# Stick-breaking attention: the values become the stationary operand, and half of the later weight copies go to another engine

## The chip, the cores and the metric

One Trainium2 chip, of which the kernel uses one core. The metric is the time of one execution in device microseconds (us), the median of several runs. Five engines work side by side, each through its own instructions in order: TensorE (PE; its weight loads are shown as PEld), VectorE (DVE), ScalarE (ACT), GpSimd (POOL) and SyncE (SP), which here only issues transfers.

## The reference

One layer: a hybrid of two sequence mixers, then a mixture of 16 experts. 512 tokens of 1024 features follow 16 meta tokens. What the change touches is the second mixer, stick-breaking attention with 8 heads of 64 features, which runs over blocks of 128 queries:

```python
def stick_breaking_mixer(q, k, v, norm_g):
    ...
    for blk in range(Lp // Q_BLOCK):
        z = jnp.einsum('bhqd,bhkd->bhqk', qh[:, :, start:end], kh[:, :, :end])
        mask = jnp.arange(end)[None, :] < (start + jnp.arange(Q_BLOCK))[:, None]
        log_keep = jnp.where(mask, jax.nn.log_sigmoid(-z), 0.0)
        log_a = jax.nn.log_sigmoid(z) + lax.cumsum(log_keep, axis=3, reverse=True) - log_keep
        a = jnp.where(mask, jnp.exp(log_a), 0.0)
        outs.append(jnp.einsum('bhqk,bhkd->bhqd', a, vh[:, :, :end]))
    o = jnp.concatenate(outs, axis=2).transpose(0, 2, 1, 3)
    return head_rms_norm(o, norm_g)
```

`head_rms_norm` divides each head's 64 features of a token by their root mean square. Both mixers' results, side by side, are multiplied by `w_out`; a layer norm, a router and the experts follow. All is float32.

## The kernel before, in words

The stages follow each other: the input projections with the first mixer (HGRN2) woven in, then the stick-breaking mixer with the output projection woven in, then the router, then the 16 experts, whose weights (96 loads of 1 MB) stream in from HBM. The large products are made in three: a float32 operand is split into a high part that TensorE takes in one pass and the low rest, and `mm3` (L126 to L130) multiplies high by high, low by high and high by low. So L128, L129 and L130 are the projections, the output projection and the experts; other products are plain float32, which the trace shows as two records for each matmul.

**The stick-breaking stage.** `UNITS` (L493) lists the work: first query block 3 alone (528 keys wide, with the meta tokens), then block 2 (400 wide), then blocks 0 and 1 together (144 + 272 = 416 wide). Heads go in pairs, four pairs `pr` for each unit. `sb_weights` (L498) makes one head's weights with queries on the partitions: `z` by TensorE, Abs, Exp and Ln on ScalarE (L518, L523, L524), a ReLU (L522), a reverse scan (L527) and a subtraction (L529) on VectorE, Exp on ScalarE (L530).

`sb_values` (L535) multiplies a pair's weights by the values. For each head it turns the 128x128 blocks of weights with TensorE (L543) into the one bank `tr`, VectorE copies them out as `aT` (L545: four blocks in the first unit, three in the others), and L550 has a block of `aT` as the stationary operand and 64 columns of values `svt` as the moving one, so that the result bank `o` holds queries on the partitions and features along the row. There are 12 such groups (three units of four pairs), 24 copies and 80 products.

`sb_finish` (L553) ends a group of heads and runs five times (for unit 1, for unit 2, and in unit 3 for the pairs 0 and 1, for pair 2, for pair 3): the meta tokens' part (L562), Square on ScalarE (L567), a sum over 64 features on VectorE (L569), Ln and Exp of 8 numbers a row on ScalarE (L570, L571), a multiplication on VectorE (L572), four transposes back to features on TensorE (L575), and in `mixed_parts` (L470) the high part on ScalarE (L477) and the low part on VectorE (L478). These feed the second half of the output projection, `wo_mm`.

**What sets the order.** `weave` (L68, called in L929) interleaves the steps of `stick_breaking` and `out_proj` by a ratio; a scheduler then lays the instructions out engine by engine, and each engine runs its own in that order. Large tiles `b` come from a ring of 14 buffers (`big`, L98): each new tile waits until the one 14 places before it is no longer used. The raw loads of `w_out` (L730, split on L736 and L737) and of the experts' weights (L894, split on L922 and L923) come from it. The PSUM bank `tr` has one buffer, the small tiles `t` have two (`T_BUFS`, L60).

## Time and profile before

| | us |
|---|---|
| median of 3 runs | 701.22 (699.14 to 703.21) |
| the profiled execution | 695.96 |
| its span, first to last instruction | 694.2 |
| stick-breaking stage in it (first of its score products to the last of its low parts) | about 236 to 348 |
| router and first expert's start | about 348 to 400 |
| experts | about 400 to 650 |

The profile gives, for each engine and stretch, how long the engine was busy; for each group of instructions how often it ran, how long one took, and the idle time of the engine before it with what ended that idle time. A record's time includes that until its result is out, so records of TensorE overlap: the distance from one start to the next tells what one costs. The profiled execution is 5.26 us shorter than the median of the runs.

### The profile page before, as it was taken

To read this page: it belongs to the slowest core of one execution; us is meant where nothing else is said; L and a number is where in the kernel's file an instruction comes from. 1 tells how busy PE (TensorE), PEld (TensorE's weight loads), DVE (VectorE), ACT (ScalarE), POOL (GpSimd) and SP (SyncE) were. 2 spreads that over 40 slices of the span, in tenths; PEclk is the share of its full clock that TensorE was granted. 3 is DMA by queue.
4 is the path that set the end of the run, shared out by engine and by line. 5 is a ranking of instruction groups with operands and counts; after the bars stand their busy time and mean duration, and the time that the engine had idled before them with its cause. 6 is when DMAs were issued, how large, how long until landed. Compare 5 with 4: busy or idle time off the path is not lost. (4 is left out here: it accounts for less than half of the span.)

```text
span 694.2 us, 9353 instructions
## 1 busy us (share of the span) xinstructions
PE 652.1 (94%) x3354; PEld 513.8 (74%) x3354; DVE 524.6 (76%) x836; ACT 412.4 (59%) x624; POOL 158.8 (23%) x177
## 2 busy tenths in 40 slices
PE   7999989999999999989978899999999999999983
PEld 6778867777778777778766678878778787787732
DVE  5353065675563796999779899999999999999484
ACT  5363333635262673855434778678688687698480
POOL 5210153343243100100001112333111141211301
PEclk9999999999999999999998999999999999999998
DMA  9532111011004880203567699999999999999641
GB/s 319 194 104 67 55 61 61 1 61 61 1 1 166 302 319 1 90 34 121 190 236 283 261 338 326 356 354 351 351 334 353 337 362 348 334 358 376 187 164 59
DMA packets 62451, 143.67 MB, mean 207 GB/s; under 512 B 7386, under 2 KB 7418, under 8 KB 62400
## 3 DMA queue, kind: packets, MB, share of 16 engines
q1 hardware_dynamic: 53312, 127.67, 50.9%
q0 software_dynamic: 5904, 12.82, 6.3%
q10 hardware_dynamic: 3184, 2.53, 1.2%
q8 instruction: 28, 0.46, 0.3%
q14 instruction: 23, 0.19, 0.1%
HBM read 137.01 MB, written 14.68 MB: 219 GB/s over the span
## 5 line engine op out<-in xcount | busy, mean ns | idle before, releaser
L923 DVE TENSOR_TENSOR b<-b 128x1024 fp32r<-128x1024 f32 x180 | 211.3, 1216 | 5.2 <-ACT b L922 5.1
L922 ACT ACTIVATE b<-b 128x1024 fp32r<-128x1024 f32 x180 | 177.6, 1054 | 7.8 <-PE pj L130 4.8
L128 PE MATMUL pj<-b 128*128 128x512 f32 x256 | 103.8, 407 | 2.3 <-ACT b L207 2.3
L129 PE MATMUL pj<-b 128*128 128x512 f32 x256 | 101.8, 397 | 0.5 <-DVE b L124 0.5
L130 PE MATMUL pj<-b 128*128 128x512 f32 x256 | 101.6, 398 | 0.0
L128 PE MATMUL pj<-b,xh 128*128 128x512 f32 x224 | 90.4, 404 | 0.2 <-ACT b L922 0.2
L129 PE MATMUL pj<-b,xl 128*128 128x512 f32 x224 | 88.2, 394 | 0.6 <-DVE xl L1243 0.6
L130 PE MATMUL pj<-b,xh 128*128 128x512 f32 x224 | 87.4, 408 | 0.8 <-DVE b L923 0.8
L124 DVE TENSOR_TENSOR b<-b 128x1024 fp32r<-128x1024 f32 x24 | 32.4, 1357 | 47.7 <-ACT b L339 44.0
L984 POOL DMA_INDIRECT xg<-h1d,idx x15 | 20.9, 1393 | 174.7 <-DVE gate L981 71.0
L128 PEld LDWEIGHTS pj<-b 128*128 128x128 f32 x256 | 48.3, 189 | 14.2 <-ACT b L207 2.6
L130 PEld LDWEIGHTS pj<-b 128*128 128x128 f32 x256 | 48.5, 190 | 10.6 <-issue 0.7
L129 PEld LDWEIGHTS pj<-b 128*128 128x128 f32 x256 | 48.6, 190 | 10.3 <-DVE b L124 0.9
L130 PEld LDWEIGHTS pj<-b,xh 128*128 128x128 f32 x224 | 42.6, 190 | 11.8 <-DVE b L923 3.1
L339 ACT ACTIVATE b<-b 128x1024 fp32r<-128x1024 f32 x28 | 29.3, 1059 | 35.6 <-PE pj L130 21.6
L1033 POOL DMA_INDIRECT ad<-y,idx x14 | 41.0, 2926 | 38.9 <-ACT b L922 30.4
L129 PEld LDWEIGHTS pj<-b,xl 128*128 128x128 f32 x224 | 42.5, 190 | 9.8 <-DVE xl L1243 1.0
L128 PEld LDWEIGHTS pj<-b,xh 128*128 128x128 f32 x224 | 42.8, 191 | 8.7 <-ACT b L922 1.5
L640 ACT ACTIVATE zs<-zs 128x512 f32<-128x512 f32 x28 | 17.7, 631 | 45.9 <-POOL zs L639 45.8
L122 POOL TENSOR_TENSOR b<-b 128x1024 fp32r<-128x1024 f32 x8 | 21.1, 2636 | 84.6 <-ACT b L339 65.6
L638 POOL TENSOR_TENSOR zs<-u 128x256 f32<-128x256 f32 x28 | 21.2, 756 | 59.5 <-issue 19.1
L641 DVE TENSOR_TENSOR zs<-zs,u 128x256 f32<-128x256 f32 x28 | 14.3, 510 | 21.7 <-ACT zs L640 21.6
(359 smaller groups left out, 1279.1 us busy)
## 6 DMA issues: line engine op xcount, KB each, us to landing
b<-in_w_exp_gate_dram SPq DMA_DIRECT2D x32, 1024.0 KB, 8.2
b<-in_w_exp_up_dram SPq DMA_DIRECT2D x32, 1024.0 KB, 10.2
b<-in_w_exp_down_dram SPq DMA_DIRECT2D x32, 1024.0 KB, 9.8
b<-in_w_in_dram SPq DMA_DIRECT2D x12, 1024.0 KB, 4.9
b<-in_w_out_dram SPq DMA_DIRECT2D x4, 1024.0 KB, 4.8
b<-in_x_dram SPq DMA_DIRECT2D x7, 512.0 KB, 7.6
b<-in_w_in_dram SPq DMA_DIRECT2D x4, 512.0 KB
h1d<-b POOLq DMA_DIRECT2D x4, 512.0 KB, 3.7
```

What stands on the lines that cost most here:

```text
L122: nc.gpsimd.tensor_sub(dst, src, hi)
L124: V.tensor_sub(dst, src, hi)
L128: nc.tensor.matmul(acc, ah, bh, start=first, stop=False)
L129: nc.tensor.matmul(acc, al, bh, start=False, stop=False)
L130: return nc.tensor.matmul(acc, ah, bl, start=False, stop=last)
L339: latest[0] = nc.scalar.activation(wt[:, 0], src, AF.Copy).ins
L638: nc.gpsimd.tensor_sub(xv[:, :, 0, :], ref, bv[:, :, 0, :])
L640: nc.scalar.activation(X, X, AF.Exp)
L922: latest[:] = (nc.scalar.activation(t[:, 0], raw, AF.Copy).ins, V.tensor_sub(t[:, 1], raw, f32(t[:, 0])).ins)
L923: V.tensor_sub(t[:, 1], raw, f32(t[:, 0])).ins)
L984: nc.gpsimd.indirect_dma_start(out=dst, out_offset=None, in_=h1d, in_offset=bass.IndirectOffsetOnAxis(ap=idx, axis=0), bounds_check=T - 1, ...
L1033: nc.gpsimd.indirect_dma_start(out=ad, out_offset=bass.IndirectOffsetOnAxis(ap=idx, axis=0), in_=y, in_offset=None, bounds_check=T - 1, oo ...
```

## The change

The operands of the products of weights and values change places. The 64 columns of values become the stationary operand and the block of `aT` the moving one. The first head's result goes to partitions 0 to 63 of `o` and the second head's to 64 to 127, so that `o` holds features on the partitions. The two heads' products alternate, in a fixed order (`issue_after`), and the first waits for the second head's copy. In the units whose groups have three blocks, the first head's copy is made by ScalarE (8 of the 24 copies). `sb_finish` copies `o` out at once into a large tile (`mixed_room`, two more tiles from the ring of 14), squares the copy, sums over a head's features by a product with `pair` (ones in two 64x64 blocks), takes Ln and Exp of whole rows, and multiplies. The four transposes back and VectorE's sum are gone.

```diff
--- before.py
+++ after.py
@@ -384,6 +384,11 @@
     skT, sqZ, svt = [], [], []
     vbd = att.tile([P, 512], F32, name="vbd")
 
+    pair = att.tile([P, P], F32, name="pair")
+    nc.gpsimd.memset(pair, 0.0)
+    for s in range(2):
+        nc.gpsimd.memset(pair[64 * s:64 * s + 64, 64 * s:64 * s + 64], 1.0)
+
     def ev_sk(c, acc):
         skT.append(att.tile([P, 528], F32, tag="skT", bufs=4, name="skT"))
         nc.scalar.activation(skT[c][:, NM:528], acc, AF.Copy)
@@ -466,6 +471,16 @@
 
     mixed = {}
     mixed_t, mixed_n = [None], [0]
+
+    rooms = []
+
+    def mixed_room():
+
+        if len(rooms) % 4 == 0:
+            rooms.append(big_tile(4))
+        else:
+            rooms.append(rooms[-1])
+        return rooms[-1][:, (len(rooms) - 1) % 4]
 
     def mixed_parts(src):
         width = src.shape[1]
@@ -534,7 +549,7 @@
 
     def sb_values(n, pr, prs, o, zz, qts, spans):
 
-        aTs = []
+        aTs, last = [], None
         blocks = [(m, j, a + NM + j * P) for m, (i, (a, b)) in enumerate(zip(qts, spans)) for j in range(i + 1)]
         w = len(blocks)
         for s in range(2):
@@ -542,13 +557,21 @@
             for n_, (m, j, a) in enumerate(blocks):
                 nc.tensor.transpose(p_[:, n_, :], zz[s][:, a:a + P], ident)
             aT = quad(tt("aT", AT_BUFS, 512))
-            V.tensor_copy(aT[:, 0:w], p_[:, 0:w])
+            if s == 0 and len(blocks) < 4:
+                nc.scalar.activation(aT[:, 0:w], p_[:, 0:w], AF.Copy)
+            else:
+                copied = V.tensor_copy(aT[:, 0:w], p_[:, 0:w])
             aTs.append(aT)
-        for s in range(2):
-            for n_, (m, j, _) in enumerate(blocks):
-                c_ = (m * len(prs) + n) * P + 64 * s
-                nc.tensor.matmul(o[:, c_:c_ + 64], aTs[s][:, n_, :], svt[j][:, (2 * pr + s) * 64:(2 * pr + s + 1) * 64],
-                                 start=(n == 0 and s == 0 and n_ == 0), stop=False, skip_group_check=True)
+        for n_, (m, j, _) in enumerate(blocks):
+            c_ = (m * len(prs) + n) * P
+            for s in range(2):
+                with tc.issue_after(last) if last else ExitStack():
+                    i_ = nc.tensor.matmul(o[64 * s:64 * s + 64, c_:c_ + P], svt[j][:, (2 * pr + s) * 64:(2 * pr + s + 1) * 64],
+                                          aTs[s][:, n_, :], start=(n == 0 and n_ == 0), stop=False, skip_group_check=True)
+                if last is None:
+                    tc.add_manual_dep(i_.ins, copied.ins.name, mybir.DependencyInfo(
+                        mybir.DependencyClass.Sync, mybir.DependencyReason.DATA), reason="both heads side by side")
+                last = i_.ins
 
     def sb_finish(am, o, prs, qts):
 
@@ -558,22 +581,23 @@
             nc.tensor.transpose(p_[:, m, :], am[:, m, :], ident)
         aMT = att.tile([P, 2 * P], F32, tag="aMT", bufs=1, name="aMT")
         V.tensor_copy(aMT[:, 0:len(qts) * P], p_[:, 0:len(qts)].rearrange("p a b -> p (a b)"))
-        for m in range(len(qts)):
-            nc.tensor.matmul(o[:, m * w:m * w + w], aMT[:, m * P:(m + 1) * P], vbd[:, prs[0] * P:prs[0] * P + w],
-                             start=False, stop=True, skip_group_check=True)
+        for n, pr in enumerate(prs):
+            for m in range(len(qts)):
+                c_ = (m * len(prs) + n) * P
+                nc.tensor.matmul(o[:, c_:c_ + P], vbd[:, pr * P:pr * P + P], aMT[:, m * P:(m + 1) * P],
+                                 start=False, stop=True, skip_group_check=True)
         n = len(qts) * w
-        heads = lambda ap: ap[:, 0:n].rearrange("p (h d) -> p h d", d=64)
-        t = tt(n=n)
-        nc.scalar.activation(t, o[:, 0:n], AF.Square)
-        rs = att.tile([P, 8], F32, tag="rs", bufs=2, name="rs")[:, 0:n // 64]
-        V.tensor_reduce(rs, heads(t), axis=AX.X, op=OP.add)
-        nc.scalar.activation(rs, rs, AF.Ln, scale=1.0 / 64.0, bias=eps_rms)
+        t, rs = tt(n=n), tt(n=n)
+
+        oc = mixed_room()[:, 0:n]
+        nc.scalar.activation(oc, o[:, 0:n], AF.Copy)
+        nc.scalar.activation(t, oc, AF.Square)
+        n_ = pj([P, n])
+        nc.tensor.matmul(n_, pair, t, start=True, stop=True)
+        nc.scalar.activation(rs, n_, AF.Ln, scale=1.0 / 64.0, bias=eps_rms)
         nc.scalar.activation(rs, rs, AF.Exp, scale=-0.5)
-        V.tensor_mul(heads(t), heads(o), rs[:, :, None].to_broadcast([P, n // 64, 64]))
-        p_ = pj([P, 4, P])
-        for j in range(n // P):
-            nc.tensor.transpose(p_[:, j, :], t[:, j * P:(j + 1) * P], ident)
-        hi, lo = mixed_parts(p_[:, 0:n // P].rearrange("p a b -> p (a b)"))
+        V.tensor_mul(rs, rs, oc)
+        hi, lo = mixed_parts(rs)
         for m, i in enumerate(qts):
             for n, pr in enumerate(prs):
                 c_ = slice((m * len(prs) + n) * P, (m * len(prs) + n + 1) * P)
```

How the instructions stand, with the tiles' buffer numbers. The first place is on TensorE at the beginning of unit 2, where unit 1 has just been finished. Before (`t` is the normalized result of unit 1, L511 and L513 the scores of the unit's third and fourth heads with their mask, `pj` their banks, `oT` the result `o`):

```order
L575 MATMUL pj_2199<-ident_75,t_2192 128x128 x4
L511 MATMUL pj_2213<-skT_1258,b_1797 128x400
L513 LDWEIGHTS identb_222
L513 MATMUL pj_2213<-maskb_223,identb_222 128x128
L511 MATMUL pj_2232<-skT_1258,b_1797 128x400
L513 LDWEIGHTS identb_222
L513 MATMUL pj_2232<-maskb_223,identb_222 128x128
L550 MATMUL oT_2245<-b_1572,aT_2250 128x64 x3
L550 MATMUL oT_2245<-b_1572,aT_2256 128x64 x3
```

In the changed kernel (L558 turns a head's weights, L526 and L528 are the scores):

```order
L558 MATMUL tr_2257<-ident_75,zs_2150 128x128 x3
L596 MATMUL pj_2204<-t_2199,pair_245 128x512
L526 MATMUL pj_2218<-skT_1262,b_1801 128x400
L528 LDWEIGHTS identb_222
L528 MATMUL pj_2218<-maskb_223,identb_222 128x128
L526 MATMUL pj_2237<-skT_1262,b_1801 128x400
L528 LDWEIGHTS identb_222
L528 MATMUL pj_2237<-maskb_223,identb_222 128x128
L569 MATMUL oT_2250<-aT_2255,b_1576 64x128
L569 MATMUL oT_2250<-aT_2261,b_1576 64x128
L569 MATMUL oT_2250<-aT_2255,b_1576 64x128
L569 MATMUL oT_2250<-aT_2261,b_1576 64x128
```

One product of 512 columns (L596) stands where four transposes stood, and the six products of the unit's first pair (L569, the last two not shown), which took their `aT` one after the other, alternate between the two heads' `aT` and have a result of 64 partitions by 128 columns.

The second place is on ScalarE, at the end of unit 2 (L530 is the Exp that ends a head's weights, L567 to L477 belong to `sb_finish`, L765 to the output projection, L262 and L263 to the layer norm after it, L518 is the Abs of a head of unit 3). Before:

```order
L530 ACTIVATE zs_2440<-zs_2440 128x416
L765 ACTIVATE b_2561<-z_2562 128x512
L567 ACTIVATE t_2480<-oT_2245 128x512
L765 ACTIVATE b_2561<-z_2568 128x512
L570 ACTIVATE rs_2482<-rs_2482,eps_rms_80 128x8
L571 ACTIVATE rs_2482<-rs_2482 128x8
L262 ACTIVATE mv_2586<-mv_2586,eps_ln_82 128x1
L263 ACTIVATE mv_2586<-mv_2586 128x1
L477 ACTIVATE b_2204<-pj_2487 128x512
L518 ACTIVATE t_2499<-pj_2494 128x416
```

In the changed kernel (L593 is the copy of `o`, L561 the copy of a head's turned weights, L594 Square, L597 and L598 Ln and Exp, L789 the output projection, L533 and L538 a head of unit 3, L492 the high part):

```order
L593 ACTIVATE b_2201<-oT_2250 128x512
L561 ACTIVATE aT_2550<-tr_2546 128x384
L594 ACTIVATE t_2488<-b_2201 128x512
L789 ACTIVATE b_2566<-z_2567 128x512
L789 ACTIVATE b_2566<-z_2573 128x512
L262 ACTIVATE mv_2591<-mv_2591,eps_ln_82 128x1
L597 ACTIVATE t_2489<-pj_2492,eps_rms_80 128x512
L263 ACTIVATE mv_2591<-mv_2591 128x1
L598 ACTIVATE t_2489<-t_2489 128x512
L533 ACTIVATE t_2504<-pj_2499 128x416
L538 ACTIVATE t_2504<-t_2504 128x416
L492 ACTIVATE b_2209<-t_2489 128x512
```

ScalarE has the copy of the bank and a copy of turned weights more between the end of unit 2 and the high part, its Ln and Exp are of 512 columns instead of 8, and the next head's Abs and Exp stand ahead of the high part.

The third place is on ScalarE too, where the second half of `w_out` is first split (L736; it falls into unit 2). Before, with the Abs (L518) of the unit's sixth head:

```order
L518 ACTIVATE t_2297<-pj_2294 128x400
L524 ACTIVATE t_2275<-t_2275 128x400
L530 ACTIVATE zs_2236<-zs_2236 128x400
L523 ACTIVATE t_2297<-t_2297 128x400
L736 ACTIVATE b_2391<-b_2389,cp_191 128x1024
```

In the changed kernel (L760 is the split, L533 the Abs of the unit's seventh and eighth heads, L538, L539 and L545 Exp, Ln and Exp):

```order
L533 ACTIVATE t_2345<-pj_2342 128x400
L545 ACTIVATE zs_2281<-zs_2281 128x400
L538 ACTIVATE t_2345<-t_2345 128x400
L545 ACTIVATE zs_2303<-zs_2303 128x400
L539 ACTIVATE t_2345<-t_2345 128x400
L533 ACTIVATE t_2358<-pj_2355 128x400
L760 ACTIVATE b_2396<-b_2394,cp_191 128x1024
```

The first split stands behind the Abs of the eighth head instead of that of the sixth.

## Rows read from the trace of the kernel before

**Rows 1.** Windows: us, busy of PE, PEld, DVE, ACT, POOL (count), PEclk, DMA share, GB/s.
```profile
236.00:258.00 22.00, 20.26 (x119) 15.81 (x117) 20.17 (x37) 18.80 (x42) 1.40 (x6) 1.00 0.96 380
258.00:282.00 24.00, 23.48 (x124) 17.71 (x125) 16.25 (x28) 10.32 (x21) 1.58 (x6) 1.00 0.00 1
282.00:339.00 57.00, 52.70 (x328) 43.38 (x328) 54.20 (x114) 37.77 (x78) 4.90 (x10) 1.00 0.26 93
348.00:400.00 52.00, 41.72 (x239) 35.01 (x238) 43.25 (x94) 26.68 (x36) 6.81 (x8) 0.93 0.69 260
400.00:650.00 250.00, 246.15 (x1197) 196.76 (x1196) 239.65 (x306) 191.56 (x227) 59.56 (x27) 0.99 0.98 343
```

**Rows 2.** Groups of instructions from 236 to 348 us, shapes apart.
```profile
L543 PE MATMUL tr<-ident,zs 128*128 128x128 f32 x80 | 13.1, 276 | 3.7 <-DVE aT L545 3.4 <-ACT t L518 0.3
...
L569 DVE TENSOR_REDUCE rs<-t 128x8 f32<-128x512 f32 x3 | 2.0, 683 | 0.1
...
L569 DVE TENSOR_REDUCE rs<-t 128x4 f32<-128x256 f32 x2 | 0.8, 400 | 0.0
```

**Rows 3.** Timeline of DVE: start us, us, instruction.
```profile
294.50 0.53 DVE L545 COPY aT<-tr 128x384 f32<-128x384 f32 x1
294.95 0.56 DVE L529 TENSOR_TENSOR zs<-pj,zs 128x400 f32<-128x400 f32 x1
...
307.94 0.69 DVE L569 TENSOR_REDUCE rs<-t 128x8 f32<-128x512 f32 x1
308.54 0.55 DVE L545 COPY aT<-tr 128x384 f32<-128x384 f32 x1
```

**Rows 4.** Timeline of PE: full-width float32 products and transposes.
```profile
279.65 1.50 PE L550 MATMUL oT<-b,aT 128*128 128x64 f32 x12
280.99 0.89 PE L511 MATMUL pj<-skT,b 128*128 128x400 f32 x2
...
306.14 1.12 PE L562 MATMUL oT<-vbd,aMT 128*128 128x512 f32 x2
307.10 0.49 PE L543 MATMUL tr<-ident,zs 128*128 128x128 f32 x3
...
309.99 0.64 PE L575 MATMUL pj<-ident,t 128*128 128x128 f32 x4
310.47 0.41 PE L511 MATMUL pj<-skT,b 128*128 128x144 f32 x2
```

**Rows 5.** Timeline of PE: products in strips of 32 and of 64 columns of the array.
```profile
24.61 0.39 PE L129 MATMUL pj<-b 128*128 128x512 f32 x1
24.84 0.39 PE L130 MATMUL pj<-b 128*128 128x512 f32 x1
25.15 1.07 PE L372 MATMUL z<-b,xm 128*32 128x512 f32 x8
26.15 0.50 PE L128 MATMUL pj<-b 128*128 128x512 f32 x1
...
129.74 0.68 PE L650 MATMUL z<-zs 128*64 128x64 f32 x8
```

**Rows 6.** Timeline of ACT: the last `sb_finish`, and the first split of `w_out`.
```profile
285.94 1.14 ACT L736 ACTIVATE b<-b,cp 128x1024 fp32r<-128x1024 f32 x1
...
344.12 0.39 ACT L567 ACTIVATE t<-oT 128x256 f32<-128x256 f32 x1 [5.88 <-PE oT L562]
...
346.72 0.38 ACT L477 ACTIVATE b<-pj 128x256 fp32r<-128x256 f32 x1 [0.99 <-PE pj L575]
```

**Rows 7.** Timeline of DVE: the multiplication of the last `sb_finish`.
```profile
345.77 0.42 DVE L572 TENSOR_TENSOR t<-oT,rs 128x256 f32<-128x256 f32 x1 [0.60 <-ACT rs L571]
```

**Rows 8.** Waits of ACT, 236 to 348 us: total us, times, longest.
```profile
ACT zs L530 <- DVE zs L529: 13.3, 12, 3.4
```

**Rows 9.** Timeline of SP: the loads of the second half of `w_out`.
```profile
244.28 41.00 SPq L730 DMA_DIRECT2D b<-in_w_out_dram  x2
```

**Rows 10.** Line L730, from the issue to the landing of its loads.
```profile
DMA to landing us min/median/max: 4.8/4.8/4.8
```

## The prediction

> **What bounds the kernel now.** I read the windows first, because the change touches one stage alone. The reader is to see that the engine at its limit is not the same from stretch to stretch [rows 1]. From 236 to 258 us (unit 1) VectorE is busy 20.17 of 22 us; from 258 to 282 TensorE 23.48 of 24, which is 97.8%, and VectorE only 16.25; from 282 to 339 (units 2 and 3) VectorE 54.20 of 57 and TensorE 52.70, so both are close to full, with ScalarE at 37.77. From 348 to 400 (router) VectorE leads with 43.25 of 52, and in the experts TensorE has 246.15 of 250 while the transfer engines are at 0.98. The granted clock is 1.00 up to 339, TensorE's upper level of 2.4 GHz, so nothing in the stage is priced at a lower one.
>
> Then the groups of this stage [rows 2]. They show who waits: TensorE's transposes L543 wait 3.4 us in all for VectorE's copies L545. So VectorE is the likelier limit of 282 to 339, with TensorE about 1.5 us behind it. A saving on one alone is worth little more than that; both must fall.
>
> **VectorE.** A record's duration is longer than what it costs: the copy that starts at 294.50 lasts 0.53 us, but the next operation starts at 294.95, so it costs 0.45 [rows 3]. In the same way a sum over 512 columns costs 0.60 (307.94 to 308.54) [rows 3]; the one over 256 has 400 ns on record against 683 [rows 2], and I put it at 0.31, less by the same overlap. Eight of 24 copies go to ScalarE, one for each pair of units 2 and 3; all five sums go. In the whole case this is 8 x 0.45 + 3 x 0.60 + 2 x 0.31 = 6.0 us by distance, or 8 x 0.55 [rows 3] + 2.0 + 0.8 [rows 2] = 7.2 by duration. In 282 to 339 lie six of the copies, two large sums and one small: 2.7 + 1.5 = 4.2 us. The multiplication and the low part stay, at the same size.
>
> **TensorE, the values.** A group of a narrow unit is 12 records now, from 279.65 to 280.99: 1.34 us, 0.112 each [rows 4]. A record has 64 moving columns and a stationary block of 128 columns, and its 12 loads set this distance. In the changed kernel the block moves (128 columns) and 64 columns are loaded, into one half of the array for the first head and the other half for the second. A pass of 512 float32 columns costs 0.43 us: the two of L562 run from 306.14 to 307.10, entry included [rows 4]. So 128 columns cost 0.107.
>
> Whether the two halves run side by side no row shows for 64 columns. The nearest is L372, whose strips are 32 columns wide: eight records of 512 columns, four strips by two passes, take 1.07 us [rows 5] where one full-width product of two passes takes 1.12 [rows 4]. The strips do run side by side. A change of shape costs something at its edges: L372 starts 0.31 after the record ahead of it, where 0.23 is usual for that stream, ends 0.10 before the next, which lasts 0.50 instead of 0.39 [rows 5]. With its own first load I put this at 0.34 for a group. The eight 64-column records of L650 last 0.68 in all, each with a load of its own [rows 5], so inside one strip a load is hidden. I count 0.02 for the second strip's later start: 0.13 a pair of records. A narrow group then costs 6 x 0.13 + 0.34 = 1.12 instead of 1.34, and a wide one (16 records, 1.79 by the same distance) 8 x 0.13 + 0.34 = 1.38. That is -0.22 and -0.41.
>
> The Trainium skill, page "TensorEngine Tiling (Array Packing)", section Performance Considerations, names this very exchange of the operands for a moving side of at most 64 columns; its Theoretical Speedup is up to two. By it alone, without the edges that rows 5 show, a group would as an estimate halve to 0.67, and TensorE would have 6 x 0.45 = 2.7 us less in the sum below.
>
> **TensorE, the finish.** Four transposes of L575 cost 0.48 us (309.99 to 310.47) [rows 4]. The product with `pair` is 512 columns in two passes, 0.96 by L562. So +0.48 in each of the three finishes with 512 columns, and +0.24 in the two with 256. L562 keeps its size in columns. In 282 to 339: 6 x (-0.22) + 2 x 0.48 + 0.24 = -0.1 us. TensorE is left where it was; what it gains is shorter waits for `aT`, since the first head's copy runs on another engine.
>
> **ScalarE.** It gets eight copies (0.5 us each, by VectorE's), a copy of `o` (0.4 to 0.6), and Ln and Exp of 512 or 256 columns instead of 8. With 37.77 of 57 us busy there is room for it in units 2 and 3 [rows 1]. I cost it at nothing there; the cover is ScalarE's idle time, and if the order put the copies behind something that waits, the price is that of the second rival.
>
> **The end of the stage.** In the last finish nothing covers the chain. Now it goes from the Square at 344.12 to the high part at 346.72, 2.60 us [rows 6]. Then: copy 0.39 and Square 0.39 (as the Square now), product about 0.65 (0.48 and its way out), Ln and Exp 0.39 each, multiplication 0.42 [rows 7], and some 0.3 for the signals: 2.95. So +0.35.
>
> **Loads and the ring.** `mixed_room` takes two of the 14 large buffers. The first load of the second half of `w_out` is now issued at 244.28 and the second only 41 us later [rows 9], when a buffer that the first half's weights held comes free. In the changed kernel the first one must wait in this way too, and at worst as long: until 285.3; it lands 4.8 us after its issue [rows 10], at 290.1. Its split, now at 285.94 [rows 6], would be 4.1 us late where it stands; but it stands two heads further down, which is 9 us at the mean pace of the stretch (six pairs in 57 us). Between 0 and 4.1 us; I take 0, the later place being its cover. On SP the experts' loads behind it move later too; the experts come after the router, so I cost that at nothing. POOL's memsets of `pair` stand at the program's start, where nobody waits for them.
>
> **The sum.** In 282 to 339 VectorE's part would give 4.2 us. TensorE's limit is (52.7 - 0.1) / 0.978 = 53.8 us, a gain of 3.2. I take 3.8 for the stretch, between the two, as shorter waits for `aT` also fall to TensorE. From 258 to 282 TensorE is full; it has one pair product more (+0.48) and a few of the wide groups (-0.41 each): about 0. Unit 1 itself keeps its copies on VectorE: 0. With the end's -0.35 the gain is 3.45 us. The router follows the stage and is bound by VectorE; the experts are full. So a shift of the stage's end passes on. The profiled execution of 695.96 us would become 692.5; it lies 5.26 below the median, and the median of 701.22 becomes **697.8**. Ends: all of VectorE's 7.2 us gives 694.0; a gain of 0.95 (the third rival) gives 700.3. About 0.5%, 3.5 us here, is what a measurement of this kernel can tell from no change, so the forecast lies at that border.
>
> **Rivals.**
> First, the halves don't run side by side. Then a narrow group costs 12 x 0.107 + 0.34 = 1.63, or +0.29. In 282 to 339 TensorE has 52.7 + 1.7 + 1.2 = 55.6, over 0.978 is 56.9: gain 0.1. Add about 1.1 in 258 to 282 (0.48 and 0.26 for each of two or three wide groups) and 0.65 at the end (the last group lies there too): **702.9**. For it: no row has two heads' records in halves of 64. Against: L372 [rows 5]. Chance 0.12.
>
> Second, on the other side: ScalarE runs in order, and a copy L561 stands behind an Exp of weights that waits for VectorE. Now these waits are 13.3 us in 12 times, 1.1 each [rows 8]. While the copy waits, the one bank `tr` stays full, the second head's transposes wait, and TensorE with all behind them. If all eight copies bring such a wait onto the path, 8.9 - 3.45 = 5.4 us are lost: **706.7**. It decides from 3.1 copies on, where the gain is eaten. For it: at the end of unit 2 the copy stands behind two Exps and the copy of `o`. Against: ScalarE's own waits are for VectorE, which gets lighter. Chance 0.16.
>
> Third, the loads into the halves aren't hidden. A half load is 0.056 (half of 0.112); a pair of records 0.186, a narrow group about 1.44, +0.10: TensorE has 52.7 + 0.6 + 1.2 = 54.5, over 0.978 is 55.7, gain 1.3, and 0.95 with the end: **700.3**. L650's records speak against it, but they lie in one strip [rows 5]. Chance 0.05. The Trainium skill, page "TensorE: Matmul & The Clock Gate", Part 3 (packing), says a load overlaps running products only when its row groups differ; the two heads share all rows. By that rule it is this rival that comes; no run here yet shows it for halves.
>
> Fourth, the gain is absorbed: the experts' transfers are at 0.98 [rows 1], and if they, not the stage's end, set the experts' pace, the time stays at **701.2**. Against: TensorE is as full, and later loads are released by buffers that the stage frees. Chance 0.07.
>
> **Numbers.** Forecast 0.60: 0.37 of it below 697.7 (faster by over 0.5%), 0.23 within. No overlap: 0.04 within, 0.08 slower. ScalarE: 0.02 within, 0.14 slower. Third and fourth: 0.12 within. Together 0.37, 0.41, 0.22. The range of 8 in 10 reaches from the forecast's lower end, 694.0, to 704.0, which takes in the no-overlap case and half of the way to ScalarE's; above it and below lie 0.2.
>
> **What would show it.** Right: records of L569 that start in pairs less than 0.05 us apart, a narrow group of about 1.1 us; the first head's L561 close behind its transposes; L558 hardly waiting for `aT`; VectorE some 4 us lighter in units 2 and 3; the last low part near 344.5 instead of 348; the experts as long as before. Wrong: a group of 1.6 us (first rival); ScalarE's L561 late behind Exp and TensorE idle at L558 for a bank (second); a stage that ends earlier and experts that take the difference (fourth); or a split L760 that waits for its load and holds the projection.

## The result, and the profile after

Over 20 runs each the changed kernel took 707.25 us in the median (701.96 to 711.49) and the kernel before 702.59: ratio 1.0073, 95% interval 1.0051 to 1.0095. (The ratios and the means over runs, here and below, take the runs in the faster state alone, and the ratios are not quotients of the medians.) It is slower by about 5 us, where 3.45 us less were forecast. The profiled execution of the changed kernel is 710.99 us (span 709.3), 3.7 above its median; that of the kernel before lies 6.6 below its own. So the two profiles are 15 us apart, three times what the medians are. Where a second profile of the same kernel differs, it is said.

The windows that answer to [rows 1], for the changed kernel:

```profile
282.00:339.00 57.00, 52.96 (x334) 39.86 (x331) 50.82 (x104) 42.15 (x89) 4.86 (x11) 0.97 0.27 96
348.00:400.00 52.00, 36.86 (x208) 30.92 (x207) 37.35 (x88) 21.42 (x32) 6.15 (x7) 0.83 0.60 224
400.00:650.00 250.00, 246.63 (x1204) 198.00 (x1203) 240.95 (x308) 196.04 (x231) 66.24 (x27) 0.99 0.98 345
```

VectorE has 3.4 us less to do in 282 to 339, as it should (4.2 were forecast), and TensorE is as busy as ever. The router is where the rows part: 52 us hold 36.86 us of TensorE where they held 41.72, at a granted clock of 0.83 instead of 0.93. In the experts TensorE is full in both.

**The stage.** One window over the whole stage, from the first Abs to the start of the last low part. Before:

```profile
234.64:347.14 112.50, 105.49 (x625) 84.08 (x623) 95.65 (x195) 69.50 (x146) 9.23 (x24) 1.00 0.40 147
```

The changed kernel:

```profile
236.27:349.95 113.68, 105.57 (x643) 77.93 (x641) 90.05 (x182) 76.24 (x159) 7.83 (x23) 0.98 0.40 147
```

The changed kernel with one edit behind the stage (`gather_late`, below; its instructions in the stage are the same):

```profile
234.92:347.39 112.47, 104.35 (x643) 76.67 (x641) 89.99 (x181) 76.28 (x159) 7.85 (x23) 1.00 0.40 148
```

Where the clock stays at 1.00, the stage is 112.50 us before and 112.47 after: nothing was gained and nothing lost. With one fall of the clock in it (0.98 and 0.99) it is 113.68 after, and 114.03 in the second profile of the kernel before. Before, TensorE is busy 105.49 of 112.50 us and VectorE 95.65: over the whole stage it is TensorE that is near its limit.

**The products of weights and values** themselves became much cheaper. TensorE's timeline, changed kernel, one group of unit 2:

```profile
281.26 0.22 PE L528 MATMUL pj<-maskb,identb 128*128 128x128 bf16 x1
281.41 0.88 PE L569 MATMUL oT<-aT,b 128*64 128x128 f32 x12
282.21 0.94 PE L526 MATMUL pj<-skT,b 128*128 128x400 f32 x2
```

Twelve records cost 0.80 us (281.41 to 282.21), where they cost 1.34 [rows 4] and 1.12 were forecast. The halves run side by side, and the loads are hidden. But they now wait, for the second head's copy; before, TensorE waited for copies at the turning, 3.4 us [rows 2], and that is gone but for 1.0. The waits of TensorE in the stage (total us, times, longest), changed kernel:

```profile
PE oT L569 <- DVE aT L563: 2.9, 4, 1.1
PE pj L519 <- DVE zs L544: 2.2, 4, 1.1
...
PE tr L558 <- ACT aT L561: 1.0, 2, 0.6
```

**Behind the stage.** The waits of TensorE from 350 us on, before:

```profile
PE z L970 <- ACTq L1133: 2.9, 1, 2.9
PE z L1054 <- DMA xg<-h1d,idx: 2.0, 1, 2.0
PE tr L818 <- DVE Mb L805: 1.7, 1, 1.7
```

and in the changed kernel:

```profile
PE z L994 <- DVEq L1157: 5.1, 1, 5.1
PE z L1078 <- DMA xg<-h1d,idx: 4.9, 1, 4.9
PE tr L842 <- DVE Mb L829: 2.6, 1, 2.6
```

These are the same three places: the branch behind expert 0, the first gathered rows (transposes L1054, now L1078), and the ranks of the router (L818, now L842). Together they are 6.6 us before and 12.6 after. The second profiles say the same: 3.8, 1.6 and 1.7 before, 4.9, 4.7 and 2.6 after. No line that the diff touches stands there. What changed is the order that the scheduler chose. In the kernel before no product stands among the eight transposes; in the changed one:

```order
L128 MATMUL pj<-b,xh 128x512
L1078 MATMUL z<-ident,xg 128x128
L130 MATMUL pj<-b,xh 128x512
L128 MATMUL pj<-b,xh 128x512
L129 MATMUL pj<-b,xl 128x512
L130 MATMUL pj<-b,xh 128x512
L1078 MATMUL z<-ident,xg 128x128 x7
```

and its timeline:

```profile
380.63 0.40 PE L128 MATMUL pj<-b,xh 128*128 128x512 f32 x1
385.93 0.47 PE L1078 MATMUL z<-ident,xg 128*128 128x128 f32 x1 [4.90 <-DMA xg<-h1d,idx]
386.06 0.77 PE L130 MATMUL pj<-b,xh 128*128 128x512 f32 x1
386.63 0.63 PE L128 MATMUL pj<-b,xh 128*128 128x512 f32 x1
387.05 0.63 PE L129 MATMUL pj<-b,xl 128*128 128x512 f32 x1
387.48 0.63 PE L130 MATMUL pj<-b,xh 128*128 128x512 f32 x1
387.91 1.56 PE L1078 MATMUL z<-ident,xg 128*128 128x128 f32 x7
```

Four products that were ready (`gather_late`, below, runs them ahead of the transposes without a wait) stand behind a transpose that waits for a transfer, and when they run at last, the clock is low: 0.43 us from one to the next instead of 0.23. They also stand ahead of the other seven transposes, so the gathered rows, ScalarE, VectorE and the branch come later in turn.

The order is not all of it. Four products of 0.23 us are 0.9 us of the 2.9 by which the wait for the gather grew. The rest is the gather itself: it was issued 26.5 us after the start of the last low part instead of 25.9, and took 9.5 and 9.3 us to land (first and second profile) where it took 8.0 and 8.4. Why the transfer took longer is not shown. The longer wait before the ranks delays nothing by itself: L818 and L842 both start 13.5 us after the last low part, and only less other work stands ahead of them.

From the last low part of the stage to the Silu of expert 0 it is 39.8 us before (347.14 to 386.95) and 43.4 after (349.95 to 393.31), and 39.5 and 43.1 in the second profiles. To the Silu of expert 1, behind the branch, it is 53.6 and 61.3 us (second profiles 54.8 and 61.2); 1.5 us of that come back by the Silu of expert 5.

The clock follows the idle time. Windows of four microseconds around these places, before:

```profile
361.00:365.00 4.00, 1.28 (x8) 1.01 (x9) 4.00 (x9) 0.88 (x1) 0.00 (x0) 0.89 0.00 0
365.00:369.00 4.00, 4.00 (x27) 4.00 (x26) 4.00 (x11) 0.60 (x1) 2.10 (x4) 0.69 0.32 129
...
381.00:385.00 4.00, 3.86 (x14) 3.44 (x15) 1.66 (x3) 2.45 (x4) 0.00 (x0) 0.57 1.05 402
...
389.00:393.00 4.00, 3.47 (x22) 2.94 (x23) 3.40 (x9) 1.35 (x2) 0.77 (x1) 1.00 0.44 147
```

and in the changed kernel, which is some 3 to 7 us later here:

```profile
364.00:368.00 4.00, 1.79 (x9) 1.41 (x10) 4.00 (x9) 0.00 (x0) 0.00 (x0) 0.50 0.00 0
368.00:372.00 4.00, 4.00 (x21) 4.00 (x20) 2.64 (x6) 1.27 (x2) 2.10 (x4) 0.50 0.34 136
...
392.00:396.00 4.00, 0.02 (x1) 0.00 (x0) 2.37 (x5) 3.77 (x4) 0.00 (x0) 1.00 0.01 2
396.00:400.00 4.00, 2.92 (x14) 2.36 (x15) 3.58 (x8) 0.00 (x0) 0.20 (x1) 0.50 0.37 114
400.00:404.00 4.00, 4.00 (x13) 3.18 (x12) 3.17 (x10) 2.12 (x2) 2.15 (x2) 0.64 1.02 379
```

TensorE idles before each fall, and works at the lower of its two levels (1.2 instead of 2.4 GHz) right after it. The wait at the branch (392 to 396) is followed by a fall, in both profiles of the changed kernel. The first profile of the kernel before has none there, but its second has one too (granted clock 0.60 in 392 to 396), so this fall doesn't belong to the changed kernel alone.

Each run has its span and mean clock; span times (1 - clock), the time by which the grant was short, is 14.6 us in the mean of 97 runs of the kernel before and 19.8 in 32 of the changed one, 5.2 more. What is left of the span is 685.4 and 685.8. So over all runs the loss goes with a lower grant; how much of it the falls cost can't be read from this sum, since it also counts falls in which TensorE stood idle.

### The profile page after: what moved, and what is told of

Its sections match the earlier page's. It is cut to its first block, busy times and chain, and to the rows that moved or that the text cites. A ratio compares the mean times of both kernels' runs of the same rounds, so it can differ in the third digit from the quotient of the medians.

```text
span 709.3 us, 9372 instructions
## 1 busy us (share of the span) xinstructions
PE 657.7 (93%) x3364; PEld 511.4 (72%) x3364; DVE 520.4 (73%) x823; ACT 419.2 (59%) x637; POOL 165.6 (23%) x180
## 5 line engine op out<-in xcount | busy, mean ns | idle before, releaser
L947 DVE TENSOR_TENSOR b<-b 128x1024 fp32r<-128x1024 f32 x180 | 211.4, 1218 | 5.5 <-ACT b L946 5.4
L946 ACT ACTIVATE b<-b 128x1024 fp32r<-128x1024 f32 x180 | 177.9, 1054 | 13.5 <-PE pj L130 11.9
L128 PE MATMUL pj<-b 128*128 128x512 f32 x256 | 105.9, 416 | 1.5 <-ACT b L207 1.4
L129 PE MATMUL pj<-b 128*128 128x512 f32 x256 | 103.2, 403 | 0.5 <-DVE b L124 0.5
L130 PE MATMUL pj<-b 128*128 128x512 f32 x256 | 103.6, 406 | 0.0
L124 DVE TENSOR_TENSOR b<-b 128x1024 fp32r<-128x1024 f32 x24 | 35.4, 1482 | 46.1 <-ACT b L339 42.6
L1008 POOL DMA_INDIRECT xg<-h1d,idx x15 | 24.6, 1641 | 157.3 <-DVE gate L1005 94.3
L128 PEld LDWEIGHTS pj<-b 128*128 128x128 f32 x256 | 49.6, 194 | 13.9 <-ACT b L207 1.6
L1057 POOL DMA_INDIRECT ad<-y,idx x14 | 45.7, 3265 | 56.4 <-ACT b L946 46.1
L129 PEld LDWEIGHTS pj<-b 128*128 128x128 f32 x256 | 49.8, 194 | 10.7 <-DVE b L124 0.9
L130 PEld LDWEIGHTS pj<-b 128*128 128x128 f32 x256 | 49.2, 193 | 11.2 <-issue 0.7
L130 PEld LDWEIGHTS pj<-b,xh 128*128 128x128 f32 x224 | 42.4, 189 | 10.9 <-DVE b L947 2.4
```

The lines of the kernel that those rows point to most:

```text
L124: V.tensor_sub(dst, src, hi)
L128: nc.tensor.matmul(acc, ah, bh, start=first, stop=False)
L129: nc.tensor.matmul(acc, al, bh, start=False, stop=False)
L130: return nc.tensor.matmul(acc, ah, bl, start=False, stop=last)
L946: latest[:] = (nc.scalar.activation(t[:, 0], raw, AF.Copy).ins, V.tensor_sub(t[:, 1], raw, f32(t[:, 0])).ins)
L947: V.tensor_sub(t[:, 1], raw, f32(t[:, 0])).ins)
```

## The experiments

Theory A was that the loss comes from the router's ranks alone, B that it is made by the new waits in the stage, C by the two large buffers; D, after the first four runs, that it is made at the first gather, and E that it is not.

**`cover_after`**: all products of `sf` between the last scores and the ranks.

```diff
-    for hf in range(2):
-        first_rows(hf, 1)
+    with tc.issue_after(score[0]):
+        for hf in range(2):
+            first_rows(hf, 1)
```

> The changed kernel with one edit: the 16 products of sf (L968 there) are held until the last scores of tokens 0 to 255 (L792), so that TensorE has 1.8 us of work while VectorE ranks; in the changed kernel 2 of the 16 stand there, before the change 6. Theory A (the loss is made in the router: less work in this gap, TensorE idle 2.6 us instead of 1.7, the granted clock down to 0.50, the gather and the first experts later): idle before the rank products about 1 us, clock near 1.00 from there to the first expert, and 3 to 5 us less than the changed kernel, ratio to the kernel before 0.999 to 1.003. Theory B (the loss is made in the stick-breaking stage by new waits, and the router only follows): no more than 1 us less than the changed kernel, ratio about 1.007. Theory C (two buffers less for the expert weights): as B.

Measured: 707.24 us, ratio 1.0110 (1.0065 to 1.0156). The wait before the ranks is gone from its profile, and the kernel takes no less than the changed one: theory A falls.

**`cover_before`**: the same edit in the kernel before.

> The kernel before with the same edit alone: all 16 products of sf (L944) between the last scores and the ranks, where 6 stood. Theory A: the gap of 1.7 us shrinks to under 1, the granted clock falls less often in the router, and the kernel is 1 to 3 us faster, ratio 0.996 to 0.999. Theories B and C: no difference, within 1 us.

Measured: 703.70 us, ratio 1.0022 (0.9983 to 1.0062). No difference that the interval shows; it agrees with the run above.

**`one_by_one`**: the heads' products one after the other, in the same halves of the array.

```diff
-        for n_, (m, j, _) in enumerate(blocks):
-            c_ = (m * len(prs) + n) * P
-            for s in range(2):
-                with tc.issue_after(last) if last else ExitStack():
+        for s in range(2):
+            for n_, (m, j, _) in enumerate(blocks):
+                c_ = (m * len(prs) + n) * P
```

> The changed kernel, but the two heads' products of weights and values no longer alternate: the first head's, then the second's, without a fixed order, the first not waiting for the second head's copy. If the halves of the array run side by side only where the heads alternate, a group of 12 records goes from 0.8 us or less to 1.4 or more, 12 groups 7 us of TensorE's time; where TensorE is the limit of the stage this costs 3 to 5 us (ratio 1.012). Theory B (the products' wait for both copies makes the loss, 2.9 us of TensorE in the stage): the waits for aT fall to under 1 us, and the time is the same as the changed kernel's or up to 2 us less. Theory A: the stage may end anywhere within 2 us of the changed kernel's, and the router keeps its loss, ratio near 1.007.

Measured: 709.50 us, ratio 1.0147 (1.0096 to 1.0198). TensorE's timeline of this kernel:

```profile
298.07 0.87 PE L568 MATMUL oT<-aT,b 128*64 128x128 f32 x6
298.87 0.49 PE L130 MATMUL z<-b 128*128 128x512 f32 x1
299.30 0.87 PE L568 MATMUL oT<-aT,b 128*64 128x128 f32 x6
```

Six records of one head alone cost 0.80 us, as much as twelve of both that alternate. So the two heads do run at the same time, and only where they alternate. The waits for copies fell to 0.7 us, yet the stage took 116.7 us instead of 112.5: theory B's remedy costs more than the wait.

**`before_again`** and **`after_again`**: both kernels once more, for a second profile.

> The kernel before once more, for a second profile: where the granted clock falls. If its falls are a matter of the order of the work, they come in the same places as in the first profile (360 to 370 and 380 to 390 us, none near 100 us, none in 300 to 310); if they differ from run to run at the same stalls, a single profile can't be set against another without taking out the falls. Ratio 1.000 within 0.002.

> The changed kernel once more, for a second profile: falls of the granted clock that the order of the work causes come again in the same places (361.9, 385.8 and 396.0 us in the first); the one near 99 us, where both kernels have the same instructions, may be missing. Ratio 1.007 within 0.003.

Measured: 701.86 us, ratio 1.0022 (0.9990 to 1.0054), and 707.93 us, ratio 1.0085 (1.0054 to 1.0116). The three waits are those given above, and the falls at the ranks, the gather and the branch come again in the changed kernel. The falls near 99 and 300 us come and go from profile to profile.

**`gather_late`**: the changed kernel; the transposes wait on TensorE until the products ahead of them in the program are issued.

```diff
-            transposed(1, big_tile(2, F32R))
+            with tc.issue_after(ended[0].ins):
+                transposed(1, big_tile(2, F32R))
```

> The changed kernel with one edit: the eight transposes of the first gathered rows (L1078, which wait for a transfer) are held on TensorE until the products of expert 0 that stand before them in the program are issued, as they stood before the change; in the changed kernel four of these products stand behind the first transpose. Theory D (the loss is made at the first gather, because the new stage makes the scheduler put work that is ready behind a transpose that waits): TensorE's wait for the gather falls from 4.9 us to 2 to 3, the wait of VectorE behind it from 5.0 to about 2, the granted clock doesn't fall a second time near 396 us, and the kernel is 3 to 4 us faster than the changed one: ratio 1.001 to 1.003. Theory E (the loss is made in the stage and in clock falls that have nothing to do with this place): within 1 us of the changed kernel, ratio 1.006 to 1.009.

Measured: 703.62 us, ratio 1.0040 (1.0008 to 1.0072), beside 707.93 us and 1.0085 for the changed kernel (`after_again`). TensorE's waits from 350 us on:

```profile
PE z L1078 <- DMA xg<-h1d,idx: 3.2, 1, 3.2
PE z L994 <- DVEq L1157: 3.0, 1, 3.0
PE tr L842 <- DVE Mb L829: 2.6, 1, 2.6
```

8.8 us instead of 12.6. This one edit of order, behind the stage, takes 4.3 us off the median, of the 5.8 by which the changed kernel was slower there; between the means it is 3.1 us (95%: 1.1 to 5.2) of 5.6. Theory E falls: the order at this place makes a good part of the loss. Theory D came true only in part. The wait for the gather fell to 3.2 us and not below 3, since the gather still landed 35.4 us after the last low part (34.0 before, 36.0 after). A fall of the clock remains at the branch, and in the mean of 12 runs the grant is still short by 18.7 us; the rest of the span is 683.8. So the edit took 2.0 us off the rest and only 1.1 off the short grant.

**`no_copy`**: Square and the multiplication read the bank; no large tiles.

```diff
-        oc = mixed_room()[:, 0:n]
-        nc.scalar.activation(oc, o[:, 0:n], AF.Copy)
+        oc = o[:, 0:n]
```

> The changed kernel without the copy of the result bank: Square and the multiplication read the bank itself, and no large tiles are taken for it. Its row of instructions at the first gather is that of the kernel before (no product behind a waiting transpose). Theory D: 3 to 4 us less than the changed kernel, ratio 1.001 to 1.003. Theory E: the stage decides; the copy was 0.4 to 0.6 us of ScalarE in each of five finishes and freed the bank earlier, so within 1 us of the changed kernel, ratio 1.006 to 1.009. If the two large tiles were the cause (the second half of w_out loaded 40 us later), the first split of w_out comes back to about 287 us and the stage's end 1 us earlier.

Measured: 701.46 us, ratio 1.0001 (0.9968 to 1.0034). Its stage is 112.77 us long, no shorter than the others; the order at the gather is the old one, and the loss is gone.

**`copy_small`**: the copy in a small tile, the ring of large buffers as before.

```diff
-        t, rs = tt(n=n), tt(n=n)
-        oc = mixed_room()[:, 0:n]
+        oc, t = tt(n=n), tt(n=n)
```

> The changed kernel with the copy of the result bank in a small tile instead of two large ones, Ln, Exp and the multiplication in place of the Square: the ring of large buffers is as before the change. At the first gather TensorE's row is that of the changed kernel, four products behind a waiting transpose. If the two large tiles made the loss (the second half of w_out and the experts' weights load later): 3 to 4 us less than the changed kernel, ratio 1.001 to 1.003. If the order at the gather makes it: as the changed kernel, ratio 1.005 to 1.009, though the first split of w_out comes 2 us or more earlier.

Measured: 707.14 us, ratio 1.0085 (1.0054 to 1.0116). Without the two large tiles the loss is all there. Its profiled execution, 702.01 us, is the shortest of its ten. In it four products do stand behind the first transpose, but it shows no loss at the gather:

```profile
PE z L992 <- DVEq L1155: 5.1, 1, 5.1
PE tr L840 <- DVE Mb L827: 2.6, 1, 2.6
PE z L1076 <- DMA xg<-h1d,idx: 1.8, 1, 1.8
```

The gather landed after 6.5 us, and TensorE waited 1.8 us for it, less than in the first profile of the kernel before. From the last low part to the Silu of expert 1 it is 56.6 us, against 57.5 in `gather_late` and 61.3 in the changed kernel. The stage, on the other hand, is 115.6 us long, 1.9 more than the changed kernel's with one fall of the clock in each; the copy now holds one of the two small tiles `t`, which may be why. So this run can't tell the order from the stage. Theory C falls by `gather_late`, which keeps both large tiles while most of the loss is gone. That the copy brings the new order is shown: every variant of the changed kernel that copies `o` has four products behind the first transpose (`gather_late` apart, whose edit moves them), and the two that don't copy it, `no_copy` and `no_copy_scalar`, have none. The first split of `w_out` started at 293.00 us, where the changed kernel has it at 292.94: it did not come earlier with the old ring.

**`before_split`**: the kernel before, with six ready products put behind the waiting transposes (`turned` is the first of these).

```diff
-                    mm3(acc[w], (xh[:, k, :], xl[:, k, :]), (sp[w][0][:, c_], sp[w][1][:, c_]),
-                        k == 0, k == KC - 1)
+                    with tc.issue_after(turned[0]) if turned[0] else ExitStack():
+                        ended[0] = mm3(acc[w], (xh[:, k, :], xl[:, k, :]), (sp[w][0][:, c_], sp[w][1][:, c_]),
+                                       k == 0, k == KC - 1)
+                if e == 0 and kk == 2 and k2 == 0:
+                    with tc.issue_after(ended[0].ins):
+                        transposed(1, big_tile(2, F32R))
```

> The kernel before with one edit that makes the order of the changed kernel worse than it has it: six products of expert 0 that are ready stand on TensorE behind the eight transposes that wait for the first gather (none stood there before, four in the changed kernel). Nothing in the stick-breaking stage differs. Theory D: TensorE's wait for the gather grows from 2.0 us by 1.4 (six products of 0.23), the first expert ends 2 us later, a further fall of the granted clock comes with it, and the kernel is 2 to 5 us slower than before, ratio 1.003 to 1.007. Theory E (this place is covered anyway): within 1 us, ratio 1.000.

Measured: 702.80 us, ratio 1.0031 (0.9996 to 1.0066). The wait grew from 2.0 to 3.2 us (1.6 in the second profile of the kernel before), near what was expected. The time points the same way, but the interval still holds no change at all: inconclusive by itself. Here all eight transposes still run ahead of the products, and the wait at the branch stays at 2.9 us.

**`all_vector`**: the changed kernel with all copies of turned weights on VectorE.

```diff
-            if s == 0 and len(blocks) < 4:
-                nc.scalar.activation(aT[:, 0:w], p_[:, 0:w], AF.Copy)
-            else:
-                copied = V.tensor_copy(aT[:, 0:w], p_[:, 0:w])
+            copied = V.tensor_copy(aT[:, 0:w], p_[:, 0:w])
```

> The changed kernel with all 24 copies of turned weights on VectorE. Its row of instructions at the first gather is that of the changed kernel. Theory D: the loss there stays. VectorE gets back 8 x 0.45 = 3.6 us in units 2 and 3; if VectorE sets the stage, it ends 2 to 3 us later, ratio 1.010; if the waits of TensorE for both copies set it, a copy on ScalarE or on VectorE is nearly the same, ratio 1.006 to 1.008.

Measured: 713.92 us, ratio 1.0175 (1.0125 to 1.0224). The whole stage, as above:

```profile
235.92:357.48 121.56, 109.03 (x645) 80.72 (x643) 94.15 (x190) 74.66 (x151) 7.62 (x23) 0.96 0.38 139
```

9.1 us longer than `gather_late`'s, for eight copies of 0.45, and slower than either case that was expected: TensorE idles 12.5 us instead of 8.1, and the clock falls with it (0.96).

**`before_scalar`**: the kernel before with the same eight copies on ScalarE, and nothing else.

```diff
-            V.tensor_copy(aT[:, 0:w], p_[:, 0:w])
+            if s == 0 and len(blocks) < 4:
+                nc.scalar.activation(aT[:, 0:w], p_[:, 0:w], AF.Copy)
+            else:
+                V.tensor_copy(aT[:, 0:w], p_[:, 0:w])
```

> The kernel before with the changed kernel's copies on ScalarE alone (8 of 24); its order at the first gather is that of the kernel before. TensorE waited 3.4 us for copies in the stage, and its waits in the stage are 5.3 us in all. If these waits are what VectorE's work costs in the stage, they fall by 2 to 3 us: ratio 0.996 to 0.998. If VectorE's busy share set the stretch as I had forecast, up to 4 us: ratio 0.994. If copies on ScalarE queue behind an Exp that waits for VectorE (second rival): 1 to 4 us slower, ratio 1.002 to 1.006.

Measured: 699.34 us, ratio 0.9969 (0.9939 to 0.9998): 2.5 us less than the kernel before, and the only one here whose interval lies below 1. The stage:

```profile
234.53:345.16 110.63, 105.82 (x625) 83.75 (x623) 91.90 (x187) 71.40 (x154) 8.52 (x24) 1.00 0.42 157
```

1.9 us shorter; TensorE idles 4.8 us instead of 7.0, and its waits for copies, 3.4 us before [rows 2], are 0.8 in sum.

**`no_copy_scalar`**: `no_copy` with both heads' copies on ScalarE in units 2 and 3.

```diff
-            if s == 0 and len(blocks) < 4:
-                nc.scalar.activation(aT[:, 0:w], p_[:, 0:w], AF.Copy)
+            if len(blocks) < 4:
+                copied = nc.scalar.activation(aT[:, 0:w], p_[:, 0:w], AF.Copy)
```

> The changed kernel without the copy of the result bank, and with both heads' copies of turned weights on ScalarE in units 2 and 3 (16 of 24). The products of the two heads side by side cost TensorE 7 us less than before in the stage, but it stands idle 9.1 us there in the kernel without the copy, 2.5 of it for the second head's copy behind VectorE's queue. If this wait is what keeps the gain from the time: it falls under 1 us and the kernel beats the kernel before, 1.5 to 2.5 us less, ratio 0.996 to 0.998. If the waits only change their place (ScalarE then has the copies behind Exp operations that wait for VectorE): ratio 1.000 to 1.004.

Measured: 703.79 us, ratio 1.0008 (0.9983 to 1.0034). The waits changed their place: 2.1 us for copies are left, and 2.4 for the scores' banks and 1.2 at the turning came or stayed.

## Why the prediction was wrong

**"VectorE is the likelier limit of 282 to 339."** This step failed, and with it "I take 3.8 for the stretch". I read the busy shares of one stretch. Over the stage TensorE leaves 7.0 us of 112.5 idle, and what VectorE is rid of shortens the stage only as far as TensorE waited for it. `before_scalar` measures that: 1.9 us for 2.2 us less idle time. In the changed kernel VectorE is rid of 5.7 us (95.65 to 89.99 in `gather_late`), TensorE's idle time rises from 7.0 to 8.1, and the stage gains 0.0 us where 3.45 were forecast: the waits of TensorE for `aT`, which I counted on to shrink, were 3.6 us and are 3.9, and those for the scores' banks went from 1.2 to 2.2.

**"TensorE is left where it was."** Right in the sum, by terms that were not. I sort TensorE's time in the stage by line, from the start of each record to the next, before against `gather_late`. The products of weights and values fell from 17.9 to 10.9 us (I had 8 x 0.22 + 4 x 0.41 = 3.4 less). The finish rose by 1.55 (L575's 1.85 became 3.40 for L596; 1.9 were forecast). But the products of the output projection rose from 44.8 to 46.6. About 1.1 of these 1.8 us lie in records directly ahead of a group in strips (up to 0.39 us instead of 0.23); the record behind costs 0.34 where it cost 0.31 before, and the rest is spread over other neighbours. Further, 1.1 us of the `sf` products moved into the stage; weights' transposes, the masks and the meta tokens' transposes took 1.3 more; and idle time rose by 1.1. The sum is -0.15, nothing.

**The values' mechanism** was right and its size too careful: 0.80 for a narrow group, not 1.12. (One reading behind the 0.34 was off: by [rows 5] L372 ends at 26.22, 0.07 us behind the next record's start at 26.15 and not 0.10 ahead of it.) The first rival (no overlap) falls by this and `one_by_one`, and so does the third: twelve records in 0.80 us leave no room for twelve loads. The Trainium skill, page "TensorE: Matmul & The Clock Gate", Part 3, has a load overlap running products only where row groups differ; here both heads share all rows and the loads are hidden, so the measurement decides against the rule in this case. The gain of "up to two" (the Trainium skill, page "TensorEngine Tiling (Array Packing)", Theoretical Speedup) came to 1.34 / 0.80, or 1.7.

**"I cost it at nothing" (ScalarE).** Right: the copies on ScalarE help, here by 6 us (`all_vector` against the changed kernel, 713.92 and 707.93) and by 2.5 in the kernel before. The second rival, on the other side, fell: TensorE waited 1.0 us for L561.

**The end of the stage.** The chain from the copy to the high part, changed kernel, ScalarE's timeline, answers to [rows 6]:

```profile
346.46 0.38 ACT L593 ACTIVATE b<-oT 128x256 f32<-128x256 f32 x1 [4.10 <-PE oT L587]
346.88 0.42 ACT L594 ACTIVATE t<-b 128x256 f32<-128x256 f32 x1
348.08 0.47 ACT L597 ACTIVATE t<-pj,eps_rms 128x256 f32<-128x256 f32 x1 [0.79 <-PE pj L596]
348.59 0.42 ACT L598 ACTIVATE t<-t 128x256 f32<-128x256 f32 x1
349.50 0.42 ACT L492 ACTIVATE b<-t 128x256 fp32r<-128x256 f32 x1 [0.49 <-DVE t L599]
```

3.04 us (346.46 to 349.50) instead of 2.60: +0.44, against +0.35.

**"A shift of the stage's end passes on."** This is the step that turned the sign. I took it that everything behind the stage stays as it is. Where the order behind stays, a shift does pass on: in `before_scalar` 1.9 us of stage became 2.5 us of time between the medians, which speaks against the fourth rival. But in the changed kernel the order behind the stage is another one, and from the last low part to the Silu of expert 1 it lost 7.7 us (6.5 in the second profiles), in a place where a transfer is waited for. `gather_late` shows that the order there makes a good part of it, and `no_copy`, which has the old order, has none of the loss. None of my rivals had it. The difference of the two orders was there to be read ahead of the result, at the first gather as in the stage; I read it only where the diff is.

**The ring** was right at 0 as far as can be seen: `gather_late` keeps the two large tiles, and TensorE waited 0.5 us for the split that came 5 us later (after the shift of 1.6 us with which the stage began).

What stays open: the 1.5 us that `gather_late` still lacks, and the short grant that it keeps; why the gather takes 6.5 us to land in one kernel and 9.5 in another; where the loss of `copy_small` lies in an execution of median length; and by which of the scheduler's estimates the copy puts one transpose ahead. That was not tried, and the reverse test, `before_split`, was inconclusive.

## What to carry to other kernels

A change to one stage can be paid for in another: compare the whole order of instructions on the bound engine, and look first at rows that wait for a transfer or a branch, for what is ready but stands behind them. Before a saving is counted on an engine, read how long the fullest engine idles over the whole stage; that idle time is the most that the others' work can give back. And split a change: here eight copies on another engine were a gain, and the larger edit beside them was not.

## What the hardware showed unexpectedly

The granted clock falls at the same stall in one execution and not in the next. Up to 102 us both kernels do the same on TensorE, with a stall of 2.0 us in 96 to 100. In the first profile of the kernel before:

```profile
96.00:98.00 2.00, 0.51 (x8) 0.00 (x0) 1.69 (x4) 1.05 (x3) 0.00 (x0) 1.00 0.59 136
98.00:100.00 2.00, 1.48 (x12) 1.31 (x13) 0.38 (x1) 0.38 (x1) 0.30 (x1) 1.00 0.99 384
100.00:102.00 2.00, 2.00 (x11) 1.62 (x10) 0.37 (x2) 0.63 (x1) 0.94 (x2) 1.00 0.03 8
```

In its second profile:

```profile
96.00:98.00 2.00, 0.62 (x8) 0.00 (x0) 1.69 (x5) 1.16 (x4) 0.00 (x0) 1.00 0.62 132
98.00:100.00 2.00, 1.37 (x10) 1.24 (x11) 0.48 (x1) 0.38 (x1) 0.20 (x1) 0.81 1.00 382
100.00:102.00 2.00, 2.00 (x7) 1.52 (x6) 0.27 (x1) 0.63 (x1) 1.04 (x2) 0.50 0.04 14
```

The same idle time, and a fall in one of them; everything behind it is 1.6 us later. Most of the spread of 8 to 10 us between runs of one kernel goes with such falls: over the 97 runs of the kernel before, the span and the time by which the grant was short have a correlation of 0.81. That is why stages are compared here between profiles with the same falls in them.
